# Stationary operands with a step of two elements in a two-layer transformer kernel

## The chip, the cores and the metric

The kernel runs on one core of one Trainium2 chip. The metric is the device time of one execution in microseconds, lower being better. Before the change three runs took 3182.39, 3182.71 and 3183.04 us; the median is 3182.71 us.

## The reference

The reference computes two decoder layers, one after the other, on 256 tokens of 2,048 features in float32. Cut to what matters:

```
# first layer
h = rmsnorm(x);  proj = h @ w_in                # q, k, v of two attentions, two gates
y_sb, y_ca = stick_breaking(...), chunked_relpos(...)
x += (sigmoid(gate_sb) * (y_sb @ w_sb_out) + sigmoid(gate_ca) * (y_ca @ w_ca_out)) @ w_mix_out
x += (silu(h @ w_gate) * (h @ w_up)) @ w_ffn_out          # h = rmsnorm(x)
x += sigmoid(h @ w_ple_gate) * (p @ w_ple_in);  x = rmsnorm(x)
# second layer
proj = rmsnorm(x) @ w_in_2                      # inputs of three branches and their gates
x += (g0 * s5(...) + g1 * gla(...) + g2 * diff_attn(...)) @ w_out_2
x += conv_gated_mlp(rmsnorm(x)); x = rmsnorm(x)
```

Nearly all arithmetic is in the products of the 256 tokens with the weight matrices.

## The kernel before

**Two parts for each number.** Each weight and each activation is split into a high part of reduced precision (type `float32r`) and the rest, a low part of the same type. A product is the sum of three: high by high, high by low and low by high. `hilo` makes the two parts of an activation tile: ScalarE copies (or scales) into the high part, VectorE subtracts it from the source.

**The stream.** `stream` runs one long list of "halves" through TensorE. A half is a tile of 128 x 1,024 weights (512 KB). SyncE's queue loads it into one of four `raw` buffers (L459), ScalarE makes its high part `wh` (L466, five buffers), four halves ahead, and VectorE its low part `wl` (L476, four buffers), three halves ahead. The jobs that the halves belong to come in two kinds.

- An activation-stationary job ("AS", `mm_as`) computes 256 tokens by 512 columns. For each of the two blocks of 128 features in a half and each 128 tokens (m = 0, 1), three matmuls run: low activation by high weights (L560), high by low (L561), high by high (L562). The activation's 128 x 128 block is stationary, the weights' 512 columns move. A half is 12 matmuls; there are 593 such halves, and one more, the very first, that runs its low-weight products last (L550 to L553).
- A weight-stationary job ("WS") computes 2 x 128 columns by 256 tokens, transposed. For each of four blocks of features and each of two weight blocks (f = 0, 1), the high weights are stationary and the activation's 512 columns, 256 high and 256 low, move (L526), and the low weights are stationary while the 256 high columns move (L530). A half is 16 matmuls; there are 492 such halves. `ws_sum` (L438) then adds the two 256-column parts of the accumulator: ScalarE copies the second out of PSUM (L441), VectorE adds the first (L442).

The products of the low and high parts accumulate in PSUM in two accumulators that jobs use in turn. Every matmul has its own weight load (LDWEIGHTS), which TensorE runs beside the matmul before it.

**The tiles.** An activation tile of `Acts` holds four blocks of features; a block is 512 elements per partition, the 256 high parts and then the 256 low parts. `at(k)` gives block k, `two(k)` two of them. A stationary block of 128 tokens is thus 128 neighbouring elements. A weight tile of a WS job holds for each block of features first the 128 columns of f = 0, then those of f = 1; `_ws` lays them out so on the host.

**The rest.** Attention, the scan, norms and gating are written as generators; `tick` advances them between halves, and their instructions stand in the engines' queues between those of the stream. Their own matmuls are plain float32 and together a small share.

Of the kernel before, what the change touches and what calls it, by code (L numbers as in the profile page):

```python
# [9 lines left out]
F32 = mybir.dt.float32  # L10
# [3 lines left out]
ALU = mybir.AluOpType  # L14
# [171 lines left out]
class Build:  # L186
# [128 lines left out]
    def hilo(self, hi, lo, src, scale=None):  # L315

        if scale is None:
            self.nc.scalar.copy(hi, src)  # L318
            self.nc.vector.tensor_sub(lo, src, hi.bitcast(F32))  # L319
# [17 lines left out]
    def to_acts(self, src, acts, n, scale=None, gcol=None):  # L337

        yield from self.open_acts(acts, n)
        banks = []  # L340
        for half in range(2):
            b = yield from self.bank()
            for kk in range(2):
                for m in range(2):
                    c = half * 256 + kk * 128
                    self.nc.tensor.transpose(b[0][:, kk * 256 + m * 128:kk * 256 + m * 128 + 128],  # L346
                                             src[:, m, c:c + 128], self.ident)
            banks.append(b)
        yield
        for half in range(2):  # L350
            k = 4 * n + 2 * half
            if gcol is None:
                t = acts.two(k)
                ps = banks[half][0].rearrange("p (k t) -> p k t", k=2)
                self.hilo(t[:, :, 0:256], t[:, :, 256:512], ps, scale)
            else:
                for kk in range(2):
                    t = acts.at(k + kk)
                    self.hilo(t[:, 0:256], t[:, 256:512], banks[half][0][:, kk * 256:kk * 256 + 256],
                              self.par[:, gcol + k + kk:gcol + k + kk + 1])  # L360
            acts.ready.update((k, k + 1))
            self.unbank(banks[half])
# [75 lines left out]
    def ws_sum(self, acc, out, rb=None, n=2):  # L438

        nc = self.nc  # L440
        nc.scalar.copy(out, acc[:, 0:n, 256:512])  # L441
        nc.vector.tensor_add(out, acc[:, 0:n, 0:256], out)  # L442
        if rb is not None:
            nc.vector.tensor_mul(out, out, rb.tile[:, None, :].to_broadcast([128, n, 256]) if n > 1 else  # L444
                                 rb.tile[:, None, :])


    def stream(self, jobs):
# [40 lines left out]
        for i, (j, idx, ks) in enumerate(halves):  # L489
# [23 lines left out]
            if j.kind == "AS":  # L513
                self.mm_as(j.acts, ks, wh, wl, acc, (0, 1), first, end, low_last=i == 0)
            elif j.kind == "W4":

                for k in range(16):
                    p = slice(32 * (k % 4), 32 * (k % 4) + 32)
                    nc.tensor.matmul(acc[p, 0, :], lhsT=wh[:, 32 * k:32 * k + 32].bitcast(F32),
                                     rhs=j.acts.at(k).bitcast(F32), start=k < 4, stop=k >= 12)  # L520
            else:
                for kk, k in enumerate(ks):
                    x = j.acts.at(k)
                    for f in range(2):
                        s = slice((kk * 2 + f) * 128, (kk * 2 + f) * 128 + 128)
                        hi = lambda: nc.tensor.matmul(  # L526
                            acc[:, f, :], lhsT=wh[:, s], rhs=x, start=k == first, stop=k == end)
                        if k == first:
                            hi()
                        nc.tensor.matmul(acc[:, f, 256:512], lhsT=wl[:, s], rhs=x[:, 0:256], start=False, stop=False)  # L530
                        if k != first:
                            hi()
# [6 lines left out]
    def mm_as(self, acts, ks, wh, wl, acc, ms, first, end, low_last=False):  # L539

        nc = self.nc
        if low_last:
            for low in (False, True):
                for kk, k in enumerate(ks):
                    s = slice(kk * 512, kk * 512 + 512)
                    for m in ms:
                        x = acts.at(k)
                        xh, xl = x[:, m * 128:m * 128 + 128], x[:, 256 + m * 128:384 + m * 128]
                        if low:
# [5 lines left out]
        for kk, k in enumerate(ks):  # L555
            x = acts.at(k)
            s = slice(kk * 512, kk * 512 + 512)
            for m in ms:
                xh, xl = x[:, m * 128:m * 128 + 128], x[:, 256 + m * 128:384 + m * 128]
                nc.tensor.matmul(acc[:, m, :], lhsT=xl, rhs=wh[:, s], start=k == first, stop=False)  # L560
                nc.tensor.matmul(acc[:, m, :], lhsT=xh, rhs=wl[:, s], start=False, stop=False)  # L561
                nc.tensor.matmul(acc[:, m, :], lhsT=xh, rhs=wh[:, s], start=False, stop=k == end)  # L562
# [37 lines left out]
    def first(self):  # L600
# [6 lines left out]
        def start(load):  # L607
# [10 lines left out]
            for k in range(16):  # L618
# [6 lines left out]
                yield from self.open_acts(XT, k // 4)  # L625
                t = XT.at(k)
                self.hilo(t[:, 0:256], t[:, 256:512], xs[k // 8][0][:, k % 8, :], self.col(P_GMIX + k))
                XT.ready.add(k)
# [43 lines left out]
        def yt_out(Y, h, b, key):  # L672

            yield from self.open_acts(Y, h // 4)
            t = Y.at(h)
            self.hilo(t[:, 0:256], t[:, 256:512], b[0][:, 0:256])
            Y.ready.add(h)
# [159 lines left out]
        def ple_start():  # L837
# [5 lines left out]
            PT.slots[0] = self.slot([128, 4, 512], F32R)  # L843
            t = PT.two(0)
            self.hilo(t[:, :, 0:256], t[:, :, 256:512], s[0])
            self.drop(s)
# [89 lines left out]
    def hidden1(self, j, kl, acc, free, hid, rb):  # L936
# [10 lines left out]
        yield  # L947
        t = hid.at(kl)
        self.hilo(t[:, 0:256], t[:, 256:512], s[:, 0])
        hid.ready.add(kl)  # L950
# [420 lines left out]
    def head_norm(self, b, t, w, acts, h, post):  # L1371
# [20 lines left out]
        for vh in range(2):  # L1392
# [4 lines left out]
            else:  # L1397
                self.stt(c, c, s1, ALU.mult, s2, ALU.mult)
        dst = acts.two(2 * h)
        self.hilo(dst[:, :, 0:256], dst[:, :, 256:512], t.rearrange("p (a t) -> p a t", a=2))  # L1400
        acts.ready.update((2 * h, 2 * h + 1))
        yield

    def hidden2(self, j, kl, acc, free, hid, rb):
# [19 lines left out]
        yield  # L1424
        h = hid.at(kl)
        self.hilo(h[:, 0:256], h[:, 256:512], c[:, 0])
        hid.ready.add(kl)
# [205 lines left out]
    def s5(self, uslot, ZT):  # L1633
# [60 lines left out]
        for j2 in range(4):  # L1694
# [33 lines left out]
            if j2 % 2:  # L1728
# [4 lines left out]
                yield from self.open_acts(ZT, g)  # L1733
                t = ZT.slots[g][0]
                yield

                for jj in range(4):
                    yt = y[:, jj].rearrange("p (t c) -> p c t", t=4)
                    hi, lo = (t[:, jj, h:h + 256].rearrange("p (c t) -> p c t", t=4) for h in (0, 256))
                    self.hilo(hi, lo, yt)  # L1740
# [27 lines left out]
```

## Time and profile before

| | |
|---|---|
| median of the runs | 3182.71 us |
| the profiled execution | 3182.36 us |
| its span, first to last instruction | 3180.2 us |
| granted TensorE clock, mean | 0.999 |
| busy: TensorE matmuls | 3161.4 us |
| busy: TensorE weight loads | 2668.2 us |
| busy: VectorE, ScalarE, GpSimd | 1994.4, 1553.3, 72.5 us |
| bytes moved by DMA | 617.90 MB, 194 GB/s in the mean |

A group's row names line, engine, operation, output and inputs, shape and count; behind the bar stand the busy time of the group in us and the mean ns of one record, and behind the second bar idle time ahead of it and what ended that. PE is TensorE's matmuls, PEld its weight loads, DVE VectorE, ACT ScalarE. Records of matmuls overlap: the busy time of a group counts overlapping time once, and the time from one matmul to the next is read from the timeline.

### The profile page before, as it was taken

Reading aid. Unit: us, or ns where it says so; the run is one execution under the profiler, and the core shown is the slowest. Engines: PE = TensorE matmul, PEld = TensorE weight load, DVE = VectorE, ACT = ScalarE, POOL = GpSimd, SP = SyncE. Lnnn points to the kernel's source line nnn. Section 1 sums busy time; section 2 is a strip of 40 time slices with the busy share of each in tenths; the row PEclk is TensorE's granted clock in tenths of the full one; section 3 lists DMA queues with packets and bytes.
Section 4 is the critical chain, followed back from the end, with each engine's and each line's share of the span. In section 5 each row is a group of like instructions: output and inputs, shape, how many; then the busy total and the mean of one; then the engine's idle time right before and its main releaser. Section 6 shows DMA issues by size and latency. Waiting matters only on the chain.

```text
span 3180.2 us, 43735 instructions
## 1 busy us (share of the span) xinstructions
PE 3161.4 (99%) x16909; PEld 2668.2 (84%) x16909; DVE 1994.4 (63%) x2593; ACT 1553.3 (49%) x2035; POOL 72.5 (2%) x158
## 2 busy tenths in 40 slices
PE   8999999999999999999999999999999999999998
PEld 7888888888888888888888888878888888888887
DVE  5656445557577676566655657945555766757666
ACT  6544444455444454456544454434445644545545
POOL 0000000000001000000000001000000000000000
PEclk9999999999999999999999999999999999999999
DMA  7555555565667767555654565655555555555554
GB/s 263 168 176 166 185 188 183 180 187 186 216 223 246 243 225 238 186 175 190 210 178 159 170 214 192 211 183 198 197 183 182 186 192 185 186 195 185 189 185 165
DMA packets 172639, 617.90 MB, mean 194 GB/s; under 512 B 23552, under 2 KB 23968, under 8 KB 169232
## 3 DMA queue, kind: packets, MB, share of 16 engines
q1 hardware_dynamic: 164992, 577.49, 55.8%
q0 software_dynamic: 7440, 37.64, 3.5%
q8 instruction: 132, 2.16, 0.3%
q14 instruction: 75, 0.61, 0.1%
HBM read 599.74 MB, written 14.25 MB: 193 GB/s over the span
## 4 chain that ended last, share of the span: by engine, by line
PE 99%; ACT 0%; DMA 0%; DVE 0%; DVEq 0%; issue 0%; SPq 0%; ACTq 0%
PE acc L526 29%; PE acc L560 17%; PE acc L562 17%; PE acc L561 17%; PE acc L530 15%; PE p L346 1%; PE p L1673 0%; PE p L1132 0%; PE p L1713 0%; PE p L906 0%; PE p L908 0%; PE p L907 0%; PE p L1716 0%; PE p L1109 0%; PE p L1128 0%; PE p L1707 0%
## 5 line engine op out<-in xcount | busy, mean ns | idle before, releaser
L476 DVE TENSOR_TENSOR wl<-raw,wh 128x1024 fp32r<-128x1024 f32 x1088 | 1320.6, 1220 | 667.1 <-PE acc L561 446.0
L466 ACT CAST wh<-raw 128x1024 fp32r<-128x1024 f32 x1088 | 1138.9, 1049 | 1110.3 <-PE acc L562 672.1
L526 PE MATMUL acc<-s,wh 128*128 128x512 f32 x3936 | 1383.8, 396 | 0.0
L530 PE MATMUL acc<-s,wl 128*128 128x256 f32 x3936 | 1090.6, 282 | 0.0
L560 PE MATMUL acc<-wh,s 128*128 128x512 f32 x2372 | 939.0, 396 | 0.8 <-DVE big L1351 0.8
L562 PE MATMUL acc<-wh,s 128*128 128x512 f32 x2372 | 930.8, 392 | 0.0
L561 PE MATMUL acc<-wl,s 128*128 128x512 f32 x2372 | 930.3, 392 | 0.0
L526 PEld LDWEIGHTS acc<-s,wh 128*128 128x128 f32 x3936 | 734.1, 188 | 164.0
L530 PEld LDWEIGHTS acc<-s,wl 128*128 128x128 f32 x3936 | 741.7, 188 | 11.0 <-issue 1.0
L562 PEld LDWEIGHTS acc<-wh,s 128*128 128x128 f32 x2372 | 445.6, 188 | 99.9
L560 PEld LDWEIGHTS acc<-wh,s 128*128 128x128 f32 x2372 | 445.9, 188 | 99.2 <-issue 1.7
L561 PEld LDWEIGHTS acc<-wl,s 128*128 128x128 f32 x2372 | 446.0, 188 | 97.5 <-issue 0.5
L442 DVE TENSOR_TENSOR s<-acc,s 128x512 f32<-128x512 f32 (+1 forms) x120 | 82.7, 689 | 271.1 <-ACT s L441 271.0
L441 ACT COPY s<-acc 128x512 f32<-128x512 f32 (+1 forms) x120 | 70.0, 584 | 195.0 <-PE acc L526 192.8
L310 ACT ACTIVATE s<-s 128x256 f32<-128x256 f32 (+4 forms) x175 | 76.6, 443 | 105.2 <-DVE s L313 38.1
L313 DVE SCALAR_TENSOR_TENSOR s<-s,conv 128x256 f32<-128x256 f32 x172 | 79.4, 482 | 3.1
L444 DVE TENSOR_TENSOR s<-s,rb 128x512 f32<-128x512 f32 (+1 forms) x104 | 71.7, 690 | 3.5
L318 ACT CAST s<-s 128x256 fp32r<-128x256 f32 (+1 forms) x104 | 45.5, 442 | 30.4 <-DVE s L946 15.3
L1630 DVE TENSOR_TENSOR s<-s,s 128x1024 f32<-128x1024 f32 x48 | 58.5, 1219 | 0.0
L310 ACT ACTIVATE s<-s,conv 128x256 f32<-128x256 f32 x86 | 47.1, 595 | 22.5 <-DVE s L444 22.5
L319 DVE TENSOR_TENSOR s<-s,s 128x256 fp32r<-128x256 f32 (+1 forms) x104 | 47.4, 458 | 14.2 <-ACT s L318 13.0
L310 ACT ACTIVATE junk<-big 128x512 f32<-128x512 f32 x48 | 30.3, 632 | 50.0 <-DVE big L925 35.5
(265 smaller groups left out, 1034.5 us busy)
## 6 DMA issues: line engine op xcount, KB each, us to landing
raw<-in_w_fin SPq DMA_DIRECT2D x176, 512.0 KB, 4.3
raw<-in_w_up SPq DMA_DIRECT2D x172, 512.0 KB, 3.9
raw<-in_w_fout SPq DMA_DIRECT2D x88, 512.0 KB, 4.2
raw<-in_w_down SPq DMA_DIRECT2D x84, 512.0 KB, 4.0
raw<-in_w_qksb SPq DMA_DIRECT2D x32, 512.0 KB, 3.6
raw<-in_w_qkca SPq DMA_DIRECT2D x32, 512.0 KB, 3.4
raw<-in_w_gsb SPq DMA_DIRECT2D x32, 512.0 KB, 4.2
raw<-in_w_gca SPq DMA_DIRECT2D x32, 512.0 KB, 4.2
```

The lines of the kernel that those rows point to most:

```text
L310: self.nc.scalar.activation(out, in_, func, scale=scale, **kw)
L313: self.nc.vector.scalar_tensor_tensor(out=out, in0=in0, scalar=scalar, in1=in1, op0=op0, op1=op1)
L441: nc.scalar.copy(out, acc[:, 0:n, 256:512])
L442: nc.vector.tensor_add(out, acc[:, 0:n, 0:256], out)
L444: nc.vector.tensor_mul(out, out, rb.tile[:, None, :].to_broadcast([128, n, 256]) if n > 1 else rb.tile[:, None, :])
L466: nc.scalar.copy(wh[:, :n] if j.kind != "W4" else wh[:, :n].bitcast(F32), raws[i][:, :n])
L476: nc.vector.tensor_sub(wl[:, :n], r[:, :n], wh[:, :n].bitcast(F32))
L526: hi = lambda: nc.tensor.matmul(acc[:, f, :], lhsT=wh[:, s], rhs=x, start=k == first, stop=k == end)
L530: nc.tensor.matmul(acc[:, f, 256:512], lhsT=wl[:, s], rhs=x[:, 0:256], start=False, stop=False)
L560: nc.tensor.matmul(acc[:, m, :], lhsT=xl, rhs=wh[:, s], start=k == first, stop=False)
L561: nc.tensor.matmul(acc[:, m, :], lhsT=xh, rhs=wl[:, s], start=False, stop=False)
L562: nc.tensor.matmul(acc[:, m, :], lhsT=xh, rhs=wh[:, s], start=False, stop=k == end)
```

## The change

Every stationary operand of the stream is read with a step of two elements (8 bytes) instead of one.

- Activations: in a block, the high parts of the two token halves take turns element by element (token 0, token 128, token 1, token 129 and so on), then the low parts in the same way. `at` and `two` now give the high and the low part with the token half as a dimension of its own; a stationary block is `x[:, m]`, 128 elements with a step of two. The moving operand of a WS job, `moving(k)`, is still 512 neighbouring elements, so its PSUM columns come in the interleaved order, and `ws_sum` reads PSUM with a step of two to restore it.
- WS weights: the host interleaves the columns of f = 0 and f = 1 (`np.stack` in place of `np.concatenate`), and the two stationary blocks are `bh[:, 0]` and `bh[:, 1]` with a step of two. Transfers and the split into parts touch the same 1,024 elements as before.
- `hilo` writes the two parts with a step of two. Where it scales two blocks at once (the 0.5-scaled merged tiles), VectorE's instruction is issued once per block, 32 in place of 16 in the program.

The order of the instructions on each engine is otherwise unchanged, and so are the moving operands' and the accumulators' access patterns on TensorE, and all DMA.

```
-    return np.concatenate([blk(a), blk(b)], axis=-1).reshape(-1, 128, 1024)
+    return np.stack([blk(a), blk(b)], axis=-1).reshape(-1, 128, 1024)
...
+    def moving(self, k):
+        return self.slots[k // 4][0][:, k % 4, :]
+
     def at(self, k):
-        return self.slots[k // 4][0][:, k % 4, :]
+
+        v = self.moving(k).rearrange("p (h t m) -> p h m t", h=2, m=2)
+        return v[:, 0], v[:, 1]
 
     def two(self, k):
-        return self.slots[k // 4][0][:, k % 4:k % 4 + 2, :]
+        v = self.slots[k // 4][0][:, k % 4:k % 4 + 2, :].rearrange("p k (h t m) -> p h k m t", h=2, m=2)
+        return v[:, 0], v[:, 1]
...
     def hilo(self, hi, lo, src, scale=None):
 
+        if len(src.shape) < len(hi.shape):
+            src = src.rearrange("p (m t) -> p m t" if len(src.shape) == 2 else "p k (m t) -> p k m t", m=2)
         if scale is None:
             self.nc.scalar.copy(hi, src)
             self.nc.vector.tensor_sub(lo, src, hi.bitcast(F32))
         else:
             self.act(hi, src, AF.Copy, scale=scale)
-            self.stt(lo, src, scale, ALU.mult, hi.bitcast(F32), ALU.subtract)
+            for k in range(hi.shape[1]) if len(hi.shape) == 4 else (slice(None),):
+                self.stt(lo[:, k], src[:, k], scale, ALU.mult, hi[:, k].bitcast(F32), ALU.subtract)
...
     def ws_sum(self, acc, out, rb=None, n=2):
 
         nc = self.nc
-        nc.scalar.copy(out, acc[:, 0:n, 256:512])
-        nc.vector.tensor_add(out, acc[:, 0:n, 0:256], out)
+        a = acc[:, 0:n, :].rearrange("p n (h t m) -> p h n m t", h=2, m=2)
+        o = out.rearrange("p n (m t) -> p n m t", m=2)
+        nc.scalar.copy(o, a[:, 1])
+        nc.vector.tensor_add(o, a[:, 0], o)
...
                 for kk, k in enumerate(ks):
-                    x = j.acts.at(k)
+                    x = j.acts.moving(k)
+                    bh, bl = (t[:, kk * 256:kk * 256 + 256].rearrange("p (c f) -> p f c", f=2) for t in (wh, wl))
                     for f in range(2):
-                        s = slice((kk * 2 + f) * 128, (kk * 2 + f) * 128 + 128)
                         hi = lambda: nc.tensor.matmul(
-                            acc[:, f, :], lhsT=wh[:, s], rhs=x, start=k == first, stop=k == end)
+                            acc[:, f, :], lhsT=bh[:, f], rhs=x, start=k == first, stop=k == end)
                         if k == first:
                             hi()
-                        nc.tensor.matmul(acc[:, f, 256:512], lhsT=wl[:, s], rhs=x[:, 0:256], start=False, stop=False)
+                        nc.tensor.matmul(acc[:, f, 256:512], lhsT=bl[:, f], rhs=x[:, 0:256], start=False, stop=False)
...
             for m in ms:
-                xh, xl = x[:, m * 128:m * 128 + 128], x[:, 256 + m * 128:384 + m * 128]
+                xh, xl = (x[:, m] for x in acts.at(k))
                 nc.tensor.matmul(acc[:, m, :], lhsT=xl, rhs=wh[:, s], start=k == first, stop=False)
                 nc.tensor.matmul(acc[:, m, :], lhsT=xh, rhs=wl[:, s], start=False, stop=False)
                 nc.tensor.matmul(acc[:, m, :], lhsT=xh, rhs=wh[:, s], start=False, stop=k == end)
```

More of the change, by code (lines that the diff above doesn't have):

```diff
@@ L354, in to_acts @@
                 ps = banks[half][0].rearrange("p (k t) -> p k t", k=2)
-                self.hilo(t[:, :, 0:256], t[:, :, 256:512], ps, scale)
+                self.hilo(*t, ps, scale)
             else:
@@ L358, in to_acts @@
                     t = acts.at(k + kk)
-                    self.hilo(t[:, 0:256], t[:, 256:512], banks[half][0][:, kk * 256:kk * 256 + 256],
+                    self.hilo(*t, banks[half][0][:, kk * 256:kk * 256 + 256],
                               self.par[:, gcol + k + kk:gcol + k + kk + 1])
@@ L519, in stream @@
                     nc.tensor.matmul(acc[p, 0, :], lhsT=wh[:, 32 * k:32 * k + 32].bitcast(F32),
-                                     rhs=j.acts.at(k).bitcast(F32), start=k < 4, stop=k >= 12)
+                                     rhs=j.acts.moving(k).bitcast(F32), start=k < 4, stop=k >= 12)
             else:
                 for kk, k in enumerate(ks):
-                    x = j.acts.at(k)
+                    x = j.acts.moving(k)
+                    bh, bl = (t[:, kk * 256:kk * 256 + 256].rearrange("p (c f) -> p f c", f=2) for t in (wh, wl))
                     for f in range(2):
-                        s = slice((kk * 2 + f) * 128, (kk * 2 + f) * 128 + 128)
                         hi = lambda: nc.tensor.matmul(
-                            acc[:, f, :], lhsT=wh[:, s], rhs=x, start=k == first, stop=k == end)
+                            acc[:, f, :], lhsT=bh[:, f], rhs=x, start=k == first, stop=k == end)
                         if k == first:
                             hi()
-                        nc.tensor.matmul(acc[:, f, 256:512], lhsT=wl[:, s], rhs=x[:, 0:256], start=False, stop=False)
+                        nc.tensor.matmul(acc[:, f, 256:512], lhsT=bl[:, f], rhs=x[:, 0:256], start=False, stop=False)
                         if k != first:
@@ L555, in mm_as @@
         for kk, k in enumerate(ks):
-            x = acts.at(k)
             s = slice(kk * 512, kk * 512 + 512)
             for m in ms:
-                xh, xl = x[:, m * 128:m * 128 + 128], x[:, 256 + m * 128:384 + m * 128]
+                xh, xl = (x[:, m] for x in acts.at(k))
                 nc.tensor.matmul(acc[:, m, :], lhsT=xl, rhs=wh[:, s], start=k == first, stop=False)
@@ L674, in yt_out @@
             yield from self.open_acts(Y, h // 4)
-            t = Y.at(h)
-            self.hilo(t[:, 0:256], t[:, 256:512], b[0][:, 0:256])
+            self.hilo(*Y.at(h), b[0][:, 0:256])
             Y.ready.add(h)
@@ L843, in ple_start @@
             PT.slots[0] = self.slot([128, 4, 512], F32R)
-            t = PT.two(0)
-            self.hilo(t[:, :, 0:256], t[:, :, 256:512], s[0])
+            self.hilo(*PT.two(0), s[0])
             self.drop(s)
@@ L947, in hidden1 @@
         yield
-        t = hid.at(kl)
-        self.hilo(t[:, 0:256], t[:, 256:512], s[:, 0])
+        self.hilo(*hid.at(kl), s[:, 0])
         hid.ready.add(kl)
@@ L1398, in head_norm @@
                 self.stt(c, c, s1, ALU.mult, s2, ALU.mult)
-        dst = acts.two(2 * h)
-        self.hilo(dst[:, :, 0:256], dst[:, :, 256:512], t.rearrange("p (a t) -> p a t", a=2))
+        self.hilo(*acts.two(2 * h), t.rearrange("p (a t) -> p a t", a=2))
         acts.ready.update((2 * h, 2 * h + 1))
@@ L1424, in hidden2 @@
         yield
-        h = hid.at(kl)
-        self.hilo(h[:, 0:256], h[:, 256:512], c[:, 0])
+        self.hilo(*hid.at(kl), c[:, 0])
         hid.ready.add(kl)
@@ L1733, in s5 @@
                 yield from self.open_acts(ZT, g)
-                t = ZT.slots[g][0]
                 yield
                 for jj in range(4):
-                    yt = y[:, jj].rearrange("p (t c) -> p c t", t=4)
-                    hi, lo = (t[:, jj, h:h + 256].rearrange("p (c t) -> p c t", t=4) for h in (0, 256))
+                    yt = y[:, jj].rearrange("p (t m c) -> p m c t", t=4, m=2)
+                    hi, lo = (t.rearrange("p m (c t) -> p m c t", t=4) for t in ZT.at(4 * g + jj))
                     self.hilo(hi, lo, yt)
```

4 lines of the change are left out of this document (1 added, 3 removed).

## The prediction

> **What bounds the kernel now.** The page's chain of waits comes first, since it names the engine whose work ends last, then the costliest groups, then single instructions in order of time.
>
> ```profile
> span 3180.2 us, 43735 instructions
> PE 3161.4 (99%) x16909; PEld 2668.2 (84%) x16909; DVE 1994.4 (63%) x2593; ACT 1553.3 (49%) x2035; POOL 72.5 (2%) x158
> PE 99%; ACT 0%; DMA 0%; DVE 0%; DVEq 0%; issue 0%; SPq 0%; ACTq 0%
> PEclk9999999999999999999999999999999999999999
> ```
>
> The chain is TensorE from end to end, at full granted clock: only the time from one matmul to the next can move the span. Almost all of it lies in five lines, whose groups, kept apart by shape, stand here with four smaller ones for comparison (mean ns of one is the number behind the comma):
>
> ```profile
> L526 PE MATMUL acc<-s,wh 128*128 128x512 f32 x3936 | 1383.8, 396 | 0.0
> L530 PE MATMUL acc<-s,wl 128*128 128x256 f32 x3936 | 1090.6, 282 | 0.0
> L560 PE MATMUL acc<-wh,s 128*128 128x512 f32 x2372 | 939.0, 396 | 0.8 <-DVE big L1351 0.8
> L562 PE MATMUL acc<-wh,s 128*128 128x512 f32 x2372 | 930.8, 392 | 0.0
> L561 PE MATMUL acc<-wl,s 128*128 128x512 f32 x2372 | 930.3, 392 | 0.0
> L688 PE MATMUL p<-s 128*128 128x256 f32 x16 | 4.7, 378 | 0.0
> L906 PE MATMUL p<-s,s 128*128 128x128 f32 x48 | 9.3, 276 | 0.0
> L1673 PE MATMUL p<-s,s 128*128 128x64 f32 x128 | 15.1, 272 | 0.0
> L560 PEld LDWEIGHTS acc<-wh,s 128*128 128x128 f32 x2372 | 445.9, 188 | 99.2 <-issue 1.7 <-DVE big L1351 1.2
> ```
>
> Matmuls overlap, so a record is longer than a matmul's share of the time. The timeline of TensorE gives that share. Two stretches of the same activation-stationary loop:
>
> ```profile
> 2825.83 0.39 PE L560 MATMUL acc<-wh,s 128*128 128x512 f32 x1
> ...
> 2828.63 0.39 PE L560 MATMUL acc<-wh,s 128*128 128x512 f32 x1
> ...
> 2831.36 0.39 PE L560 MATMUL acc<-wh,s 128*128 128x512 f32 x1
> ...
> 2834.08 0.39 PE L560 MATMUL acc<-wh,s 128*128 128x512 f32 x1
> ```
>
> ```profile
> 2828.63 0.19 PEld L561 LDWEIGHTS acc<-wl,s 128*128 128x128 f32 x1
> ```
>
> From the first row to the second are 12 matmuls in 2.80 us, 233.3 ns each; from the third to the fourth 12 in 2.72 us, 226.7 ns each. A record of 392 to 396 ns is thus the interval plus about 164 ns of tail, and this difference is the same in the other groups: 378 means 214 ns, 282 means 118, 276 means 112, 272 means 108.
>
> Two things are to be seen. First, a plain f32 matmul of 256 columns (L688) takes 214 ns, though it too loads 128 new weights each time, while the stream's 512 columns take 228 to 232. I take both for 512 array cycles, the stream's columns one per cycle and the plain f32 ones one per two, at 2.4 cycles per ns: 213.3 ns (an estimate from L688's 214, and L906, half of it in columns, has 112). Then L688 adds 1 ns, the stream 13 to 20. Second, that addition takes two values a step apart, for identical instructions: 226.7 ns is 544 cycles, 233.3 is 560, or 32 and 48 beyond 512. I paired all stream matmuls of the trace with the built program's addresses (15,000 in order). In the activation-stationary loop 3,648 intervals in which the next stationary operand and the current moving one start at the same address modulo 256 bytes have a mean of 227.2 ns; the 3,309 others 232.6 to 233.3. The two stretches above are such a pair: 128 bytes apart, and 0. The weight load for L561 starts when the L560 ahead of it starts (both rows at 2828.63), so the two reads walk through memory together. A cost that depends on the addresses of the two is a collision of the two reads.
>
> **The change part by part.** (1) *The stationary reads.* 14,988 stream matmuls (3,936 twice, 2,372 three times) get a stationary operand whose 128 columns lie 8 bytes apart instead of 4. How the load and the moving read then meet isn't in the trace of before, since no stationary operand there has a step. What can be worked out: the moving read advances 4 bytes a cycle (512 columns in 512 cycles). A load has about 107 ns (L1673, whose 64 columns would need less, still takes 108, so the load is what it waits for), so 128 columns in some 256 cycles: 2 bytes a cycle now. The moving read overtakes the load by 512 bytes while it lasts, two or three times past a pattern that repeats every 256 bytes: 32 or 48 cycles are two or three collisions of 16. With a step of two the load walks at 4 bytes a cycle too. The two keep their distance and cannot overtake: either no collision, or one at the start. That is also how the plain f32 matmuls stand (both reads at 2 bytes a cycle), and these have 1 ns to spare at most.
>
> Lower bound of the new interval, by the nearest rows: 378 ns records for 512 columns (L688), and 275 for the 256 columns of L530, where the next load (L906, L1673: 272 to 276) then binds. The gain is at most
> L526: 3,936 x (396 - 378) = 70.8 us;
> L560 to L562: 2,372 x (18 + 14 + 14) = 109.1 us;
> L530: 3,936 x (282 - 275) = 27.6 us; together 207.5 us.
> Upper bound on the side of a loss: 32 cycles is also one per 16 bytes of a 512-byte column row; if each 16-byte piece costs one cycle, a step of two reads 64 pieces, and each interval grows by 32 cycles, 13.3 ns: 14,988 x 13.3 = 199 us of loss. Between them I take the walk at equal speed, because the cost depends on the distance of the two addresses, which a price per piece doesn't explain, and because the f32 rows, with equal speeds, lack it. Of the four distances seen (0, 64, 128 and 224 modulo 256) I let one in four pay one collision of 16 cycles (6.7 ns): 14,988 / 4 x 6.7 = 25 us kept. Net gain 207.5 - 25 = 182 us. All of it lies on the chain, as TensorE is 99% of it.
>
> The Trainium skill ("TensorE: Matmul & The Clock Gate", section "Step-by-step: what each phase is for") says that TensorE has two independent read ports and that loading the next weights takes no read bandwidth from the running matmul. By that rule nothing would change. The two stretches above disagree: equal instructions differ by 6.6 ns with their addresses. The Trainium skill ("SBUF — State Buffer", section "Door 1") has 16-byte lines, of which a stream should use two hits or more; a step of two in f32 has just two, so by that note the load itself stays as quick, which no run here shows yet.
>
> (2) *The copies around it.* The order of instructions is the same on every engine; VectorE has 16 more. ScalarE and VectorE now write the two parts of an activation, and read a weight-stationary sum, with a step of 8 bytes. Nothing (the step is free) is one bound; the other is the nearest rows with a step, the gelu outputs, which are read 256 bytes apart:
>
> ```profile
> 2169.58 1.22 ACT L318 CAST s<-s 128x256 fp32r<-128x256 f32 x2
> 2170.26 1.18 DVE L319 TENSOR_TENSOR s<-s,s 128x256 fp32r<-128x256 f32 x2 [0.83 <-ACT s L318]
> L318 ACT CAST s<-s 128x256 fp32r<-128x256 f32 x95 | 40.0, 425 | 15.9 <-DVE s L946 15.3 <-DVE s L1423 0.4
> L319 DVE TENSOR_TENSOR s<-s,s 128x256 fp32r<-128x256 f32 x95 | 41.2, 436 | 8.7 <-ACT s L318 7.5 <-DMA conv<-in_conv 1.2
> L442 DVE TENSOR_TENSOR s<-acc,s 128x512 f32<-128x512 f32 x119 | 82.3, 692 | 269.5 <-ACT s L441 269.5
> 2649.20:2784.60 135.40, 135.40 (x769) 117.92 (x768) 98.99 (x137) 74.61 (x103) 1.13 (x11) 1.00 0.58 186
> ```
>
> That is 0.61 against 0.43 us on ScalarE and 0.59 against 0.44 on VectorE per 256 columns: up to 0.15 for a hidden tile and 0.31 for a sum (L442) on VectorE. The stage that loads VectorE most is the up projection with the convolution: 12 jobs in 135.4 us, VectorE 99.0 (the third pair; TensorE and its loads stand ahead of it). It gets 12 x 0.46 = 5.5 us at most, and the stage shrinks by 384 pairs x 25 ns = 9.6 us to 125.8: 104.5 of 125.8, 83%. So TensorE covers it; were that cover gone, the 120 sums and some 200 tiles would cost about 120 x 0.31 + 200 x 0.15 = 67 us on VectorE. I take 0 on the path. VectorE and ScalarE spend their idle time on TensorE:
>
> ```profile
> ACT wh L466 <- PE acc L562: 672.1, 424, 3.2
> DVE wl L476 <- PE acc L561: 446.0, 297, 3.6
> GB/s 263 168 176 166 185 188 183 180 187 186 216 223 246 243 225 238 186 175 190 210 178 159 170 214 192 211 183 198 197 183 182 186 192 185 186 195 185 189 185 165
> ```
>
> They are ahead of it, held by buffers that it frees. What is late next would be the weight transfers: 512 KB per half, 8 pairs x 327 ns = 2.62 us or 12 x 214 = 2.57, so 200 to 204 GB/s; the trace has slices of 238 to 263.
>
> (3) *16 more VectorE instructions*: the 0.5-scaled tiles are split in two, 16 x (2 x 0.48 - 0.68) = 4.5 us, under TensorE. Host layout costs no device time.
>
> The sum: 3180.2 - 182 = 2998, plus the 2.2 us by which the profiled execution (3182.36) exceeds its span: **3000 us**; the median before, 3182.71, is 0.35 above that execution, which changes nothing.
>
> **The rivals.** *Collisions stay* (nothing happens): the cost belongs to handing over weights, whatever their step, and the address only shifts it. For it: the 32 cycles are there at every distance. Against it: f32 matmuls hand over weights for 1 ns. 3182 us. *A price per 16-byte piece*: the loss above, on every stream matmul. For it: exactly 32 = 512 / 16 at the best distance. Against it: 48 at others, and 24 to 27 over 256 columns (118 ns). 3182 + 199 = 3381 us; it decides once a load costs more pieces than overtaking did, 32 to 48. It is the rival on the slower side, together with its cousin: *the load itself slows* to twice its 107 ns. The 512-column matmuls (228 ns) would still hide 214, but after L530's 118 the load would bind: 3,936 x (219 - 118) = 398 us, 3580. Against that: nothing in the trace shows a load of another length, except with fewer columns. *Half the way*: a first collision in most matmuls, 14,988 x 6.7 = 100 us kept of 207.5: 3075, still faster.
>
> **How the numbers follow.** Forecast with its half-way case 0.63, no change 0.14, price per piece 0.16, slower load 0.07. The likeliest case's own range is 2960 to 3080: nothing kept gives 3182.4 - 207.5 = 2975, 15 us less if L530's next load binds later than L906's does (4 ns x 3,936), and 3075 is the half-way case. The whole range also takes in the unchanged case and losses up to 1%, and leaves out the two slower rivals' full prices: 2960 to 3215. A measurement tells 0.2%, 6 us, from no change; faster 0.63, same 0.14, slower 0.23.
>
> **What would show it.** Right: L526 and L560 to L562 records near 380 ns, L530 near 275, the loads still near 188, and equal intervals at all distances. Records of 405 to 410 would be the price per piece, loads near 290 the slower load, both unchanged the first rival. If the five lines shrink and the span doesn't, idle time before L560 and L526, released by DVE or ACT, would show that the copies took over.

## The result and the profile after

The changed kernel takes **3210.47 us** (median of 4, 3209.74 to 3211.82), the kernel before, on the same chip, 3182.88 (3182.39 to 3183.16): a ratio of 1.0087, 95% interval 1.0070 to 1.0105. The forecast was 3000 us and faster; it became slower by 28 us. The profiled execution took 3210.8 us with a span of 3208.2.

Span, busy TensorE and chain of waits of the changed kernel's page:

```profile
span 3208.2 us, 43751 instructions
...
PE 3189.6 (99%) x16909; PEld 2751.7 (86%) x16909; DVE 1996.2 (62%) x2609; ACT 1557.5 (49%) x2035; POOL 72.1 (2%) x158
...
PE 99%; ACT 0%; DMA 0%; DVE 0%; DVEq 0%; issue 0%; SPq 0%; ACTq 0%
```

TensorE is still the whole chain, and its busy time grew by 28.2 us (3161.4 to 3189.6), the span by 28.0. No other engine took over; the matmuls themselves take longer. Which ones, the costliest groups of the changed kernel show (L538 and L542 are the former L526 and L530, L570 to L572 the former L560 to L562), with one of its groups of weight loads:

```profile
L538 PE MATMUL acc<-s,wh 128*128 128x512 f32 x3936 | 1388.3, 397 | 0.0
L542 PE MATMUL acc<-s,wl 128*128 128x256 f32 x3936 | 1090.0, 282 | 0.0
L570 PE MATMUL acc<-wh,s 128*128 128x512 f32 x2372 | 944.7, 398 | 0.8 <-DVE big L1357 0.8
L571 PE MATMUL acc<-wl,s 128*128 128x512 f32 x2372 | 936.3, 395 | 0.0
L572 PE MATMUL acc<-wh,s 128*128 128x512 f32 x2372 | 936.2, 395 | 0.0
...
L571 PEld LDWEIGHTS acc<-wl,s 128*128 128x128 f32 x2372 | 462.4, 195 | 88.5 <-issue 0.5
```

The records of the activation-stationary lines went from 396, 392 and 392 to 398, 395 and 395 ns, L526's from 396 to 397, L530's stayed at 282. The loads went from 188 to 195.

Mean intervals from one matmul to the next, over the trace's matmuls paired in order with the built program's addresses, as in the prediction, are finer than whole nanoseconds (intervals that end at a matmul outside the stream, or are far longer than the rest, are left out):

| | before, ns | after, ns | matmuls | difference, us |
|---|---|---|---|---|
| activation-stationary, 512 columns | 229.96 | 233.12 | 7,116 | +22.5 |
| weight-stationary, 512 columns | 233.06 | 234.56 | 3,936 | +5.9 |
| weight-stationary, 256 columns | 117.99 | 117.64 | 3,936 | -1.4 |

The sum is 27.0 of the 28.0 us. Sorted by *distance* (the address at which the next stationary operand starts, minus that of the current moving one, modulo 256 bytes), the activation-stationary rows say where the loss sits. Before, 52% of these intervals had distance 0 and 227.2 ns, all the others about 233. After, distances 0 and 4 have 233.8, and 64, 128 and 224 have 230.9, 231.5 and 233.6. So the cheap case is gone: some 3,700 x (233.8 - 227.2) = 24 us. TensorE's timeline shows it in the last job, which has distance 0 throughout before, and 0 and 4 in turn after. Before and after, the first matmul shown and the one 120 later:

```profile
3132.82 0.39 PE L560 MATMUL acc<-wh,s 128*128 128x512 f32 x1
...
3160.02 0.39 PE L560 MATMUL acc<-wh,s 128*128 128x512 f32 x1
```

```profile
3159.39 0.40 PE L570 MATMUL acc<-wh,s 128*128 128x512 f32 x1
...
3187.65 0.40 PE L570 MATMUL acc<-wh,s 128*128 128x512 f32 x1
```

That is 27.20 us before, 226.7 ns each, and 28.26 after, 235.5 each. The prediction read the 226.7 as 32 cycles of cost still to be removed. For this change it was the good case, to be lost.

### The profile page after: what moved, and what is told of

Same layout as the page of the kernel before. It is cut to its first block, busy times and chain, and to the rows that moved or that the text cites. A ratio compares the mean times of both kernels' runs of the same rounds, so it can differ in the third digit from the quotient of the medians.

```text
span 3208.2 us, 43751 instructions
## 1 busy us (share of the span) xinstructions
PE 3189.6 (99%) x16909; PEld 2751.7 (86%) x16909; DVE 1996.2 (62%) x2609; ACT 1557.5 (49%) x2035; POOL 72.1 (2%) x158
## 4 chain that ended last, share of the span: by engine, by line
PE 99%; ACT 0%; DMA 0%; DVE 0%; DVEq 0%; issue 0%; SPq 0%; ACTq 0%
PE acc L538 29%; PE acc L570 17%; PE acc L572 17%; PE acc L571 17%; PE acc L542 15%; PE p L356 1%; PE p L1677 0%; PE p L1138 0%; PE p L1717 0%; PE p L913 0%; PE p L915 0%; PE p L914 0%; PE p L1720 0%; PE p L1115 0%; PE p L1134 0%; PE p L1711 0%
## 5 line engine op out<-in xcount | busy, mean ns | idle before, releaser
L478 ACT CAST wh<-raw 128x1024 fp32r<-128x1024 f32 x1088 | 1139.0, 1049 | 1129.9 <-PE acc L572 701.7
L538 PE MATMUL acc<-s,wh 128*128 128x512 f32 x3936 | 1388.3, 397 | 0.0
L542 PE MATMUL acc<-s,wl 128*128 128x256 f32 x3936 | 1090.0, 282 | 0.0
L570 PE MATMUL acc<-wh,s 128*128 128x512 f32 x2372 | 944.7, 398 | 0.8 <-DVE big L1357 0.8
L572 PE MATMUL acc<-wh,s 128*128 128x512 f32 x2372 | 936.2, 395 | 0.0
L538 PEld LDWEIGHTS acc<-s,wh 128*128 128x128 f32 x3936 | 762.5, 195 | 137.1
L542 PEld LDWEIGHTS acc<-s,wl 128*128 128x128 f32 x3936 | 773.2, 196 | 9.6 <-issue 1.0
L570 PEld LDWEIGHTS acc<-wh,s 128*128 128x128 f32 x2372 | 462.3, 195 | 90.8 <-issue 1.7
L572 PEld LDWEIGHTS acc<-wh,s 128*128 128x128 f32 x2372 | 462.3, 195 | 90.5
L571 PEld LDWEIGHTS acc<-wl,s 128*128 128x128 f32 x2372 | 462.4, 195 | 88.5 <-issue 0.5
L454 DVE TENSOR_TENSOR s<-acc,s 128x512 f32<-128x512 f32 (+1 forms) x120 | 82.7, 689 | 272.4 <-ACT s L453 272.4
L453 ACT COPY s<-acc 128x512 f32<-128x512 f32 (+1 forms) x120 | 70.0, 584 | 196.1 <-PE acc L538 193.8
L327 ACT CAST s<-s 128x256 fp32r<-128x256 f32 (+1 forms) x104 | 47.9, 464 | 30.5 <-DVE s L953 15.4
L328 DVE TENSOR_TENSOR s<-s,s 128x256 fp32r<-128x256 f32 (+1 forms) x104 | 47.6, 461 | 15.0 <-ACT s L327 13.8
```

The lines of the kernel that those rows point to most:

```text
L453: nc.scalar.copy(o, a[:, 1])
L454: nc.vector.tensor_add(o, a[:, 0], o)
L478: nc.scalar.copy(wh[:, :n] if j.kind != "W4" else wh[:, :n].bitcast(F32), raws[i][:, :n])
L538: hi = lambda: nc.tensor.matmul(acc[:, f, :], lhsT=bh[:, f], rhs=x, start=k == first, stop=k == end)
L542: nc.tensor.matmul(acc[:, f, 256:512], lhsT=bl[:, f], rhs=x[:, 0:256], start=False, stop=False)
```

## The experiments

Each experiment is compared with runs of the kernel before on the same chip as its own. Two theories stood at the start. *Distance*: the time of a matmul follows from the distance and the step, and the change turned the best case (distance 0, step one) into an ordinary one. *Step*: a step of two costs by itself, whatever the distance.

**One half of the change each.** The first kernel interleaves the weight blocks alone:

```diff
-    return np.concatenate([blk(a), blk(b)], axis=-1).reshape(-1, 128, 1024)
+    return np.stack([blk(a), blk(b)], axis=-1).reshape(-1, 128, 1024)
...
+                    bh, bl = (t[:, kk * 256:kk * 256 + 256].rearrange("p (c f) -> p f c", f=2) for t in (wh, wl))
-                            acc[:, f, :], lhsT=wh[:, s], rhs=x, start=k == first, stop=k == end)
+                            acc[:, f, :], lhsT=bh[:, f], rhs=x, start=k == first, stop=k == end)
```

> Only the two weight blocks of a weight-stationary half take turns element by element; activations, hilo and ws_sum stay as before. Distance theory (each stream matmul pays 32 to 48 cycles for the next weight load, and how many is set by the distance of the two read addresses modulo 256 bytes; step two only changes which distances are dear): by the intervals of the two traces the 512-column matmul of this loop went from 233.1 to 234.6 ns and the 256-column one from 118.0 to 117.6, so 3936 x 1.1 = +4 us, 3187 us. Load theory (step two makes the load itself 7 ns longer, 188 to 195 in the records, and the matmul behind it waits): 3936 x 7 = +28 us, 3210 us. Copy theory (the loss comes from copies with a step on ScalarE and VectorE): none here, 3183 us.

The second is the changed kernel without those lines: the activations alone are interleaved, with all the copies that write them and the sums that read them.

> Only the activations are interleaved (with hilo and ws_sum), weights of the weight-stationary halves lie as before. Distance theory: the activation-stationary interval went from 230.0 to 233.1 ns, because distance 0 no longer costs 227 but 234: 7116 x 3.15 = +22 us, 3205 us. Load theory as the whole cause: 7116 x 7 = +50 us, 3233 us. Copy theory: all of the loss, 3210 us.

Measured: 3189.16 us against 3183.33 (ratio 1.0017, 1.0008 to 1.0026) for the weights, and 3205.98 (1.0070, 1.0056 to 1.0083) for the activations. The losses, 5.8 and 22.7 us, add up to 28.5, against 27.6 for the whole change. The groups, of the weights' kernel and then of the activations':

```profile
L526 PE MATMUL acc<-s,wh 128*128 128x512 f32 x3936 | 1389.2, 398 | 0.0
...
L561 PE MATMUL acc<-wl,s 128*128 128x512 f32 x2372 | 930.0, 392 | 0.0
```

```profile
L538 PE MATMUL acc<-s,wh 128*128 128x512 f32 x3936 | 1385.5, 397 | 0.0
...
L571 PE MATMUL acc<-wl,s 128*128 128x512 f32 x2372 | 935.6, 394 | 0.0
```

Each half moved almost only the loop whose stationary operand it touches: with the weights interleaved the activation-stationary interval stayed at 229.96 ns and the weight-stationary one of 512 columns went from 233.06 to 234.93; with the activations interleaved they are 232.97 and 233.55. All that changes for VectorE and ScalarE belongs to the second half (the weights come interleaved from the host), and of its 22.7 us the 3.01 ns by which its activation-stationary interval exceeds before's, times 7,116, make 21.4. Little is left for the copies.

**Only the addresses.** This kernel has before's instructions, step one. Four small tiles are allocated ahead of the activation tiles, which moves these to the place modulo 256 bytes at which the weight buffers start: distance 0 everywhere. The lines that do it:

```diff
+        self.par = self.one.tile([128, P_N], F32, tag="par", name="par")
+        self.cst = self.one.tile([128, C_N], F32, tag="cst", name="cst")
+        self.tri0 = self.one.tile([128, NF2 * 8], F32, tag="more", name="tri")
+        self.nv0 = self.one.tile([128, 4], F32, tag="nvfirst", name="nvfirst")
...
```

> The kernel before with steps of one, and only the place of four small tiles in memory changed (allocated first), so that every activation tile starts at the same address modulo 256 bytes as every weight tile; no instruction differs. Distance theory: all activation-stationary intervals become 227.2 ns instead of 230.0 in the mean, 7116 x 2.8 = 20 us gained; in the weight-stationary loop 512 columns 234.0 instead of 233.1 and 256 columns 116.9 instead of 118.0, which cancel: 3163 us. If addresses have nothing to do with it (the 226.7 and 233.3 ns stretches differ for another reason, such as the place in the schedule): 3183 us.

Measured: **3164.26 us** against 3183.33, ratio 0.9938 (0.9925 to 0.9950). It is faster than both kernels. Its groups:

```profile
L532 PE MATMUL acc<-s,wh 128*128 128x512 f32 x3936 | 1385.7, 397 | 0.0
...
L568 PE MATMUL acc<-wh,s 128*128 128x512 f32 x2372 | 923.7, 389 | 0.0
L567 PE MATMUL acc<-wl,s 128*128 128x512 f32 x2372 | 923.1, 389 | 0.0
```

The activation-stationary interval fell from 229.96 to 226.98 ns: 7,116 x 2.98 = 21.2 us gained; the weight-stationary pair gained 1.0 on its 256 columns and lost 1.6 on its 512, 2.3 us. The sum, 18.9, is all of the span's difference, 18.7 (3180.2 to 3161.5). That addresses alone move this kernel's time is thereby shown: no instruction differs.

**The change, with the same move.** The changed kernel with those four tiles ahead has distance 0 or 4 everywhere. Distance alone, whatever the step, would give it the best case back.

> The changed kernel with the four small tiles moved as in e3, so that every activation and weight tile starts at the same address modulo 256 bytes: distance 0 (or 4, for the second of two interleaved blocks) throughout. Distance theory, with the step-two intervals at distances 0 and 4 as the changed kernel's own trace has them (233.8 ns in the activation-stationary loop against 233.1 in its mean, 233.6 against 234.6 and 117.2 against 117.6 in the weight-stationary one): 7116 x 0.7 - 3936 x 1.4 = about 0, 3210 us; the place that gained 20 us at a step of one gains nothing. If a common place is worth 20 us whatever the step: 3190 us.

Measured: 3214.35 us against 3183.12, ratio 1.0098 (1.0083 to 1.0113).

```profile
L577 PE MATMUL acc<-wl,s 128*128 128x512 f32 x2372 | 937.9, 395 | 0.0
```

The same alignment that gives 389 ns at step one gives 395 at step two; the mean interval is 234.06. The step does take the cheap case away. Starting 4 bytes on isn't the whole reason, though it costs by itself: at step one, distance 4 has 232.4 ns (`fine_one_b` of the third small kernel below). But the half of this kernel's operands that has distance 0 exactly takes 234.2.

**The change at its best distance.** After's own trace had its shortest activation-stationary intervals at 64 bytes. The changed kernel with the four tiles moved as before, and also 192 unused bytes ahead of the weight buffers, has 64 or 68 there, and 192 or 196 in the weight-stationary loop:

```diff
+        pool("pad", 1).tile([128, 48], F32, tag="pad", name="pad")
...
```

> The changed kernel with distance 64 (and 68) in all of the activation-stationary loop and 192 (196) in the weight-stationary one, by 192 unused bytes ahead of the stream's buffers. Distance theory, from the changed kernel's own trace: 230.75 instead of 233.1 ns, 7116 x 2.4 = 17 us gained; 235.5 instead of 234.6 and 118.4 instead of 117.6, 3936 x 1.7 = 7 us lost: 3200 us. If step two costs a fixed amount at any place: 3210 us.

Measured: 3213.73 us, ratio 1.0096 (1.0079 to 1.0113): a miss.

```profile
L545 PE MATMUL acc<-s,wh 128*128 128x512 f32 x3936 | 1413.0, 403 | 0.0
...
L578 PE MATMUL acc<-wl,s 128*128 128x512 f32 x2372 | 930.8, 392 | 0.0
```

The activation-stationary loop came out as expected (230.1 ns, records 392). The weight-stationary 512 columns took 240.3 where after's trace had 235.5 at the same distance of 192, which took 19 us back. So the distance of the next load alone doesn't settle a matmul's time in that loop. Nor does the place in memory. The changed kernel's own trace has two stretches of that loop, at distances 192 and 196, in which the operands of each matmul have the same addresses to the byte:

```profile
2575.16 0.40 PE L538 MATMUL acc<-s,wh 128*128 128x512 f32 x1
...
2576.60 0.40 PE L538 MATMUL acc<-s,wh 128*128 128x512 f32 x1
```

```profile
2744.16 0.40 PE L538 MATMUL acc<-s,wh 128*128 128x512 f32 x1
...
2745.57 0.40 PE L538 MATMUL acc<-s,wh 128*128 128x512 f32 x1
```

Four pairs of 512 and 256 columns take 1.44 us in the first and 1.41 in the second, 360 and 353 ns a pair; the 512 columns alone 242 and 235. What else settles it is open.

**Step one, aligned badly.** The kernel before with the four tiles moved and 128 unused bytes ahead of the weight buffers: distance 128 in both loops, step one.

> The kernel before with steps of one, small tiles moved as in e3 and 128 unused bytes ahead of the stream's buffers: distance 128 in both loops. Distance theory, by the intervals at distance 128 in the trace of before: activation-stationary 232.6 instead of 230.0, 7116 x 2.6 = +19 us; weight-stationary 230.4 instead of 233.1 and 119.3 instead of 118.0, 3936 x 1.35 = -5 us: 3196 us. If a common place of all tiles is worth 20 us, whatever the distance: 3164 us.

Measured: 3199.48 us against 3183.06, ratio 1.0051 (1.0037 to 1.0065).

```profile
L533 PE MATMUL acc<-s,wh 128*128 128x512 f32 x3936 | 1383.5, 394 | 0.0
L537 PE MATMUL acc<-s,wl 128*128 128x256 f32 x3936 | 1096.4, 284 | 0.0
...
L568 PE MATMUL acc<-wl,s 128*128 128x512 f32 x2372 | 935.8, 395 | 0.0
```

The activation-stationary interval is 232.40 ns, the weight-stationary ones 230.84 and 120.06, each within 0.8 ns of what was expected. A kernel of before's instructions is thus 35 us slower or faster by where its tiles lie (3199.48 and 3164.26), which is more than the change cost.

**What the addition is.** Four kernels compute no layer at all; they give their input back and run blocks of 16 to 48 stream-like matmuls, each with its own load. In the names, `one`, `two`, `four` and `eight` are the stationary operand's step, and the letters a to p are distances of 0, 16, ... 240 bytes:

```diff
+            nc.tensor.matmul(acc[0:cols, i % 2, 0:n], lhsT=st, rhs=rhs, start=True, stop=True)
```

The first varies the stationary columns (the load's length), the steps of both operands, and the type:

> No layers are computed: the kernel runs blocks of 16 stream-like matmuls, each with its own stationary operand, and varies one thing at a time; its output is the input, cast. The records' mean ns, minus about 164, is the interval. Distance theory: 512 columns, step one: record 391 at distance 0 and 397 at 64, 128, 224; step two: 395 to 398 at nearly all distances; so records go up and down with the distance, with period 256 bytes. Collision theory (the part above 378 is read collisions during the load): with 64 stationary columns half of the addition goes, record about 387, with 32 columns a quarter. Hand-over theory (a fixed cost of exchanging weights in this type): 391 to 397 whatever the number of stationary columns. The plain f32 blocks: 378 at all distances and steps by the collision theory with equal speeds only at step one; 378 throughout if the half-rate moving read leaves room.

Its groups of matmuls, then of loads:

```profile
L50 PE MATMUL full_one_i<-T 128*128 128x512 f32 x16 | 3.9, 395 | 0.0
L50 PE MATMUL full_two_i<-T 128*128 128x512 f32 x16 | 3.9, 394 | 0.0
L50 PE MATMUL cols_thirtytwo_one_i<-T 128*32 128x512 f32 x16 | 3.8, 392 | 0.0
L50 PE MATMUL half_one_i<-T 128*128 128x256 f32 x16 | 2.1, 281 | 0.0
L50 PE MATMUL half_four_i<-T 128*128 128x256 f32 x16 | 4.0, 399 | 0.0
L50 PE MATMUL plain_one_a<-T 128*128 128x256 f32 x32 | 7.1, 379 | 0.0
L50 PE MATMUL plain_two_a<-T 128*128 128x256 f32 x32 | 7.1, 379 | 0.0
L50 PE MATMUL mvtwo_one_a<-T 128*128 128x512 f32 x16 | 7.6, 649 | 0.0
```

```profile
L50 PEld LDWEIGHTS full_one_i<-T 128*128 128x128 f32 x16 | 3.0, 188 | 0.7
L50 PEld LDWEIGHTS full_two_i<-T 128*128 128x128 f32 x16 | 3.1, 196 | 0.6
L50 PEld LDWEIGHTS full_four_i<-T 128*128 128x128 f32 x16 | 3.9, 310 | 0.0
```

A load of a quarter of the columns has a quarter of the time in which it could be overtaken, yet the matmul keeps 392 ns of 395. That speaks against the prediction's collisions. Plain f32 has 379 at both steps. Its loads take 190 ns at step one and 197 at step two, so at step two they walk at nearly twice the moving read's speed, and nothing is added: equal speeds are not what spares it. A stationary step of four is where a load does cost: 310 ns, and records of 256 columns behind it go from 281 to 399. A *moving* operand with a step of two takes 649 ns, 453 from one to the next, twice a usual interval. Blocks of 256 columns alone cost 2 ns more at step two, 119.9 against 118.1 in the mean over 16 distances.

The second kernel varies the moved columns, with loads of 32 columns (`narrow`), and distances over 256 bytes (`far`):

> No layers are computed: blocks of 16 stream-like matmuls (24 in pairs of 512 and 256 columns), one thing varied at a time; the output is the input, cast. Question: does the addition beyond one column per cycle belong to each matmul (hand-over) or to each moved column (the moving read is slower than a column per cycle)? With 64 to 512 moved columns: hand-over theory, records grow by 0.417 ns per column, 53 ns per 128, with the same addition of 13 to 20 ns at every length down to where the load binds (interval 112 ns, and earlier with 32 stationary columns); column theory, they grow by 0.44 to 0.455 ns per column, 57 to 58 ns per 128. Period theory: distances 256, 512 and 1024 equal distance 0 (391), 384 and 640 equal 128 (395). Pairs: the sum of a pair at step two is never under the best at step one.

```profile
L50 PE MATMUL n_fivetwelve_narrow_i<-T 128*32 128x512 f32 x16 | 3.8, 392 | 0.0
L50 PE MATMUL n_oneninetytwo_narrow_i<-T 128*32 128x192 f32 x16 | 1.6, 252 | 0.0
...
L50 PE MATMUL far_threeeightyfour<-T 128*128 128x512 f32 x16 | 3.9, 395 | 0.0
L50 PE MATMUL far_fivetwelve<-T 128*128 128x512 f32 x16 | 3.8, 389 | 0.0
```

320 columns more take 140 ns more, 0.44 ns or 1.05 cycles a column. From one matmul to the next are 229.7 ns with 512 columns and 89.3 with 192; less one cycle a column (0.417 ns), 16 ns are added to 512 columns and 9 to 192. So most of the addition grows with the columns moved: a straight line through the two leaves 5 ns at no column. A fixed hand-over of weights, the first rival's reason, would leave 16 at both. 384 bytes behave as 128, 512 as 0: the pattern repeats every 256 bytes. (Blocks of 64 and 128 columns are left out: the granted clock was 0.50 there.) Pairs of 512 and 256 columns, the weight-stationary loop's mix, took 350.2 ns at step one and 352.8 at step two in the mean over 16 distances, and none at step two (348.9 and more) was under the best at step one, 346.9.

The third takes all 16 distances at both steps, and lets the moving operand repeat the same few columns (`fresh`: how many differ):

> No layers are computed: blocks of 48 stream-like matmuls of 512 columns, one thing varied at a time; the output is the input, cast. (1) All 16 distances in steps of 16 bytes, steps one and two: if step two only moves the dear and cheap distances about, both means over the 16 are the same, 394 in the records, and each has cheap ones near 391; if step two costs something of its own, its mean is higher by 3 or more. (2) The same with 32 stationary columns at step one: if the spread with distance is made by reads of the load colliding with those of the matmul over their whole length, it shrinks to a quarter; if it is made where the two begin, it stays. (3) The 512 moved columns taken from 256, 128 ... 2 different ones, repeated: if the extra 1 in 16 cycles of each column is the reading of fresh 64-byte pieces, it shrinks once 16 or fewer columns repeat (records towards 378); if it belongs to the type's rate in the array, it stays at 391 to 395.

```profile
L53 PE MATMUL full_one_a<-T 128*128 128x512 f32 x48 | 11.0, 389 | 0.0
L53 PE MATMUL full_one_i<-T 128*128 128x512 f32 x48 | 11.4, 395 | 0.0
L53 PE MATMUL full_two_a<-T 128*128 128x512 f32 x48 | 11.4, 394 | 0.0
L53 PE MATMUL narrow_one_c<-T 128*32 128x512 f32 x48 | 11.6, 401 | 0.0
...
L53 PE MATMUL fresh_sixtyfour_a<-T 128*128 128x512 f32 x48 | 11.1, 389 | 0.0
L53 PE MATMUL fresh_sixteen_a<-T 128*128 128x512 f32 x48 | 11.8, 405 | 0.0
L53 PE MATMUL fresh_eight_a<-T 128*128 128x512 f32 x48 | 10.6, 379 | 0.0
```

Intervals at step one are 226.7, 226.7 and 227.1 ns at distances 0, 16 and 240, and 228.9 to 234.2 at the other thirteen, mean 231.6. At step two they are 229.9 to 233.4, mean 232.3, and no distance is as cheap as 227. On an average over distances the step costs 512 columns 0.7 ns, and in this kernel, which sat at the cheap distance half the time, it cost more. With loads of 32 columns at step one (`narrow`) the intervals run from 228.9 to 239.1 ns: the spread over the distances does not shrink with the load, so it isn't made by reads that collide over the load's whole length. The addition all but vanishes when the moving read stays on 8 columns (379, as plain f32; 217.2 from one to the next), and is there as usual from 64 on. In between, at 32 and 16, it is larger (records of 400 and 405 at distance 0), which isn't explained.

The fourth keeps the load on one place (`held`: all its columns read the same element), so that nothing walks beside the moving read, and pairs the eight repeated columns with loads of both steps:

> No layers are computed: blocks of 48 matmuls of 512 columns as before; the output is the input, cast. One thing is new: the 128 (or 32) stationary columns are all the same element (a step of zero), so that the load reads one place only. If the addition beyond 512 cycles is the moving read meeting the reads of the load, it nearly goes: records near 378 to 384 at most distances and no pattern over the distance. If the addition is the moving read's own (fresh memory at one column per cycle), it stays at 389 to 396, whatever the load reads. The blocks whose moving operand repeats 8 elements, with loads of step one and two at four distances: 379 in all by both.

```profile
L53 PE MATMUL held_one_a<-T 128*128 128x512 f32 x48 | 11.3, 394 | 0.0
L53 PE MATMUL held_one_b<-T 128*128 128x512 f32 x48 | 11.0, 389 | 0.0
...
L53 PE MATMUL eightfresh_two_a<-T 128*128 128x512 f32 x48 | 10.6, 379 | 0.0
```

A load that does not walk at all leaves 394 ns (231.0 to 231.8 from one to the next) at 15 of 16 distances, with 128 and with 32 columns. A walking load isn't needed for the addition. Walking loads of either step without a walking moving read give 379 at all four distances tried. The walking moving read is needed.

## Why the prediction was wrong

**What bounds the kernel** was right: TensorE is 99% of the chain before and after, and the change in its matmuls' intervals is the change in time.

**The step that failed is in (1): "a cost that depends on the addresses of the two is a collision of the two reads", and so 32 or 48 cycles were "two or three collisions of 16" that end once the load "cannot overtake".** Three things were wrong in it.

First, most of the addition isn't the load's. It stays with a load of a quarter of the columns (392 against 395) and with one that doesn't walk (394), grows with the columns moved, and all but goes when the moving read stays on 8 columns (379). No stationary step that was tried (0, 1, 2, 3, 4 and 8) brought the mean of a block of 512 fresh columns under 226.7 ns, 13.4 beyond the 213.3 of the prediction's one column per cycle; 9.5 of these go when the columns repeat (217.2). That floor alone takes (3,936 + 7,116) x 13.4 = 148 us out of the 207.5 us that the prediction counted as the greatest gain.

Second, the f32 rows were read as a sign that equal speeds remove the cost. L688 differs from the stream in another way, which the prediction itself names: it moves a column every two cycles. With unequal speeds it still has 379. A comparison in which two things differ was taken for one. (Its intervals were also read a little short, as records less 164 ns: by the timeline L688 has 215 rather than 214, and most of L1673's are 111 to 112 rather than 108. That changes the sum little.)

Third, the dependence on the distance was real (alone worth 35 us between the best and the worst placement tried), but it was read as a variation of a cost, and no term asked what the *cheap* distance would become. The prediction's own numbers held the loss: 3,648 intervals at 227.2 ns, the others at 233. Had step two merely brought distance 0 up to the others, 3,648 x 6 = 22 us would be lost, which is near what happened. The "one collision" that one matmul in four was to keep paying, 25 us, was set against the gain instead. None of the rivals was this case. The measured 3210.47 us lies inside the range of 2960 to 3215 only because the range took in losses up to 1%; no term of the sum gave a loss, so that is luck.

**The two read ports.** The rule of the Trainium skill ("TensorE: Matmul & The Clock Gate", section "Step-by-step: what each phase is for") that loading takes no read bandwidth from the running matmul holds better than the prediction allowed: loads of 32, 128 or of one repeated element leave an addition of 13 to 26 ns each, and it is no smaller for the short ones. It doesn't cover the last 7 ns, which move with the two addresses. The load's own price came as the Trainium skill ("SBUF — State Buffer", section "Door 1"), with its 16-byte lines and two hits a line, had it: 188 to 195 ns at step two, and 310 at step four, with one hit (the same note calls a stride of four fp32 free, which the 310 does not bear out). For the moving operand the measurement differs from that note: step two, two hits, doubles the interval.

**(2) The copies** cost nothing on the path, as said. The sums (L453, L454), which read PSUM and write with a step, and the hidden tiles (L327, L328) of the changed kernel:

```profile
L454 DVE TENSOR_TENSOR s<-acc,s 128x512 f32<-128x512 f32 x119 | 82.3, 692 | 270.9 <-ACT s L453 270.8
L453 ACT COPY s<-acc 128x512 f32<-128x512 f32 x119 | 69.7, 586 | 194.0 <-PE acc L538 193.8
L327 ACT CAST s<-s 128x256 fp32r<-128x256 f32 x95 | 42.0, 446 | 16.0 <-DVE s L953 15.4 <-DVE s L1428 0.4
L328 DVE TENSOR_TENSOR s<-s,s 128x256 fp32r<-128x256 f32 x95 | 41.4, 439 | 9.2 <-ACT s L327 8.1 <-DMA conv<-in_conv 1.1
...
ACT wh L478 <- PE acc L572: 701.7, 435, 3.2
```

692 ns is unchanged, and 446 and 439 stand against 425 and 436, far below the bounds of 0.31 and 0.15 us. ScalarE still waits for TensorE (701.7 us against 672.1). **(3) The 16 instructions** and the copies together raised VectorE's busy time by 1.8 us (1994.4 to 1996.2; the prediction had 4.5 for the instructions alone), under a TensorE that stayed 99% busy.

**The rivals.** A price per 16-byte piece, 3381 us, is refuted: step two reads twice the pieces, and over all distances costs 512 columns 0.7 ns, not 13.3. The slower load, 3580, too (195, not 290). "Collisions stay" came nearest with 3182, but its reason, a hand-over cost, fits at most the 5 ns that do not grow with the moved columns. Of the marks that the prediction set, records near 380 and 275 did not come; nor did its "equal intervals at all distances", though in the activation-stationary loop after's are closer together (230.7 to 233.8) than before's (227.2 to 233.3). That step two evens the distances out was right for that loop, but it evened them at the dear end; the weight-stationary 512 columns are not evened (233.3 to 238.2, before 230.4 to 234.0).

What stays open: what makes up the part that follows the distance, why a held load is dear at 0 and cheap at 16 bytes, why 16 repeated columns cost more than 64, and why the weight-stationary 512 columns took 235 and 242 ns at the same addresses.

## What to carry to other kernels

When identical instructions take two times, look first at which of the two the change would move to the other: a cheap case may be all there is to lose. Before an access pattern is changed, sort the intervals by where the operands lie to each other; here moving four small allocations was worth 0.6%, and the change of pattern cost 0.9%. And a comparison row proves a cause only if it differs in that one thing; a block of matmuls in which the suspect stands still would have told before.

## What was not expected of the hardware

- No block of 512-column float32r matmuls with their own loads had a mean under 226.7 ns here, except when the moving read repeated 8 columns or fewer: 379 ns records, 217.2 from one to the next.
- Where the stationary operand starts relative to the moving one, modulo 256 bytes, moves that time by up to 7 ns. The absolute place alone didn't: blocks at distance 0 whose two operands both start 0, 64, 128 or 192 bytes further on all came to 226.7 ns, but three of them only after ten intervals of 224 to 236.
- A step in the operand is cheap or dear by which operand it is: stationary 188, 196, 310 and 330 ns a load at steps one, two, four and eight; moving at step two, 453 ns an interval.
